# Memory results gated in the banks and summed by accumulating stores, VectorE's order written out around a chunk's sums, branch gates loaded by GpSimd

## The chip, the cores and the metric

The kernel runs on one core of one Trainium2 chip. The metric is the device time of one launch in microseconds (us). Before the change it is 2192.47 us, the median of 3 runs (2190.98 to 2194.52).

## The reference, cut to what matters

One layer for 512 positions of width 2048: a projection `h @ w_in` whose columns feed three branches, each with an output projection; the three results are weighted by sigmoid gates, added, projected once more and added to x.

```python
h = rms_norm(x, norm_g[l])
proj = h @ w_in[l]
(c_gate, b_gate, u, conv_z, c_q, c_kv, k_rope_raw, mla_z,
 mem_q, mem_z, g_conv, g_mla, g_mem) = jnp.split(proj, split_at, axis=-1)
conv_y = b_gate * causal_depthwise_conv(c_gate * u, conv_w[l])
o_conv = (conv_y * jax.nn.silu(conv_z)) @ w_conv_out[l]
mla_y = mla_attention(c_q, c_kv, k_rope_raw, cos, sin, ...)
o_mla = (mla_y * jax.nn.silu(mla_z)) @ w_mla_out[l]
mem_y = memory_attention(mem_q, mem, mem_norm_g[l], w_mem_kv[l], mem_qn_g[l], mem_kn_g[l])
o_mem = (mem_y * jax.nn.silu(mem_z)) @ w_mem_out[l]
merged = (jax.nn.sigmoid(g_conv) * o_conv + jax.nn.sigmoid(g_mla) * o_mla
          + jax.nn.sigmoid(g_mem) * o_mem)
x = x + merged @ w_o[l]
```

Everything is float32. The memory branch attends to 256 memory tokens with 4 heads; w_mem_out is 1024 x 2048, w_mla_out and w_o are 2048 x 2048.

## The kernel before

**Products.** Each float32 product is made of three matmuls (`mm3`, L158-163): weights and data are split into a high and a low part, and high x high, high x low and low x high are added up in a PSUM bank. ScalarE (ACT) writes the high part of a weight chunk, `whi`, and VectorE (DVE) the low part, `wlo = raw - whi` (L154, L155). A chunk of raw weights is a DMA of 512 KB issued by SyncE (SP). There are three `raw` buffers and two each of `whi` and `wlo`, so splits run one or two chunks ahead of the matmuls. `take()` hands out a split chunk and begins the next ones; `queue` lists all chunks of the program in order.

**Panels.** w_h, w_mla_out and w_o run as panels (`panel_steps`): 2 x 2 blocks with seven products in place of eight. VectorE first forms three sums of each raw chunk (L263-265), ACT and DVE then split seven blocks at once (`128x1792`, L268, L269). The data side needs the same: `pair_sums` (L243-246) and `pair_split` (L249 on ACT, L250 on DVE) turn a pair of 128-row blocks into a tile `xp`, `xm` or `xo`. A panel holds four banks and takes four chunks; at its end its banks are added up into a tile `e` (L304-314) and its finish function runs. w_h has 62 panels; w_mla_out and w_o have 8 each. w_mem_kv, conv_out and w_mem_out run as plain products (`dense_units`), in groups of four banks (two in w_mem_out's last two groups).

**Stages of the run**: to 106 us keys and values of the memory (w_mem_kv, with parts of x prepared beside it); to about 1343 the panels of w_h, with the rotary work at 1005 to 1025; to 1640 the latent attention; to 1700 the memory attention woven with conv_out by a table of letters (`ORDER_MEM`; `w` is a unit of conv_out); to 1735 the rest of conv_out and the splits of xm; to 1907 the panels of w_mla_out; to about 1996 w_mem_out; then w_o.

**Gates.** The sigmoid gates lie in a DRAM buffer `gdram`. conv_out's results are multiplied by their gates (`conv_result`, L1040) and stored to `mgdram` (L1041); `gate_blocks` loads the gates for it, called just before the products. w_mla_out's results are multiplied by theirs (L1217) and added to `mgdram` by an accumulating store of GpSimd (POOL), L1218; the gates `sg` for it are loaded by SP in `middle()`, which runs after `take()` of a panel's third chunk, along with the blocks `am` for w_mem_out. In w_o's panels `middle()` loads a piece of x, `xr`; at a panel's end (`finish_o`) VectorE adds to it and ACT stores it.

**Memory results** (`mem_pair`, L1231-1241): w_mem_out's five groups give eight pairs of banks. For each pair there is one tile `mg`, with a single buffer. POOL loads the gate into one half (L1233) and the merged sum of the other branches from `mgdram` into the other (L1234); VectorE multiplies the banks into the gate (L1236, two), adds (L1237), forms the pair's sums and splits (L250) into `xo`. The generator is advanced once per so many matmul units; the order on PE and SP is the order of the program text, while VectorE's, ACT's and POOL's orders are set by a scheduler, except in a region marked `manual_schedule`; before, that was VectorE in the first six chunks of w_h.

## Time and profile before

The profiled execution took 2187.3 us; its span is 2185.5 us.

| what | value |
|---|---|
| times of three runs | 2190.98, 2192.47, 2194.52 us |
| profiled execution | 2187.3 us, span 2185.5 us, mean granted clock 0.992 |
| instructions | 38852 |
| ScalarE busy | 1003.8 us |
| GpSimd busy | 123.9 us |
| DMA | 334.31 MB, mean 153 GB/s |

Spans, windows and waits are times of one profiled execution. In a window's row each engine has its busy time in that stretch, and behind it the mean TensorE clock that the throttle granted (1.00 is full) and the share of time that the 16 DMA engines were busy. A row of the waits says which engine and line waited, for what, for how long in all, how often, and the longest one. A row of a group gives its busy time and mean duration, then how long its engine sat idle before it and what ended that.

### The profile page before, as it was taken

What the parts mean: (1) busy time and instruction counts of PE and PEld (TensorE: products, weight loads), DVE (VectorE), ACT (ScalarE), POOL (GpSimd) and SP (SyncE); (2) the same over time, 40 slices, a digit from 0 to 9 for tenths busy, and PEclk for the clock granted to TensorE, in tenths of its full rate; (3) what the DMA queues carried; (4) which work ended last, traced back from release to release, by engine and by line L of the source; (5) the groups of instructions that cost most, each with busy time, mean ns of one, the idle gap of its engine ahead of it and who ended that gap; (6) DMA issues with size and microseconds to landing.
All of it is one profiled execution on the core that took longest, in us unless ns stands there. A gap on an engine that the chain in (4) does not pass through costs nothing.

```text
span 2185.5 us, 38852 instructions
## 1 busy us (share of the span) xinstructions
PE 2128.3 (97%) x16040; PEld 2038.7 (93%) x16040; DVE 1741.5 (80%) x2764; ACT 1003.8 (46%) x1219; POOL 123.9 (6%) x173
## 2 busy tenths in 40 slices
PE   9989999999999999999999999999999999998799
PEld 8789999999999999999999999888888799987799
DVE  6986888888888888888888786888877688757787
ACT  6743444344334334444444444877764433323333
POOL 0000000000000000000000001221211100000000
PEclk9999999999999999999999999999999999999899
DMA  8633433333334334343444446222266765554343
GB/s 331 231 106 136 155 136 126 126 126 129 123 126 137 115 129 137 118 141 127 136 136 139 133 136 244 74 82 108 98 231 249 306 186 173 170 204 149 126 147 136
DMA packets 92289, 334.31 MB, mean 153 GB/s; under 512 B 10768, under 2 KB 11024, under 8 KB 90064
## 3 DMA queue, kind: packets, MB, share of 16 engines
q1 hardware_dynamic: 72000, 256.77, 34.4%
q0 software_dynamic: 11616, 51.12, 6.6%
q10 hardware_dynamic: 8496, 23.94, 3.1%
q8 instruction: 125, 2.05, 0.4%
q14 instruction: 52, 0.43, 0.1%
HBM read 273.34 MB, written 58.46 MB: 152 GB/s over the span
## 4 chain that ended last, share of the span: by engine, by line
PE 81%; DVE 8%; DMA 4%; issue 4%; ACT 2%; POOL 0%; SPq 0%; DVEq 0%; POOLq 0%; ACTq 0%
PE acc L161 14%; PE acc L162 14%; PE acc L163 14%; PE aux L163 11%; PE aux L162 11%; PE aux L161 11%; DVE wlo L269 3%; DMA raw<-in_w_mla_out 1%; DMA raw<-in_w_o 1%; DVE raw L263 1%; PE aux L978 1%; DMA sb<-gdram 1%; DMA raw<-in_w_h 1%; PE aux L961 1%; DVE wlo L155 0%
## 5 line engine op out<-in xcount | busy, mean ns | idle before, releaser
L268 ACT ACTIVATE whi<-raw 128x1792 fp32r<-128x1792 f32 x304 | 517.7, 1703 | 793.0 <-PE acc L162 352.8
L269 DVE TENSOR_TENSOR wlo<-raw,whi 128x1792 fp32r<-128x1792 f32 x304 | 614.3, 2021 | 194.2 <-ACT whi L268 193.7
L163 PE MATMUL aux<-xp,wlo 128*128 128x256 f32 (+1 forms) x1712 | 479.5, 280 | 5.0 <-DVE wlo L269 5.0
L161 PE MATMUL aux<-xp,whi 128*128 128x256 f32 (+1 forms) x1712 | 479.8, 280 | 1.0 <-ACT whi L268 1.0
L162 PE MATMUL aux<-xp,whi 128*128 128x256 f32 (+1 forms) x1712 | 480.0, 280 | 0.0
L163 PE MATMUL acc<-xp,wlo 128*128 128x256 f32 x1680 | 469.4, 279 | 3.4 <-DVE wlo L269 3.4
L162 PE MATMUL acc<-xp,whi 128*128 128x256 f32 x1680 | 469.8, 280 | 0.0
L161 PE MATMUL acc<-xp,whi 128*128 128x256 f32 x1680 | 469.3, 279 | 0.0
L163 PEld LDWEIGHTS aux<-xp,wlo 128*128 128x128 f32 (+1 forms) x1712 | 320.4, 187 | 5.6 <-DVE wlo L269 5.6
L161 PEld LDWEIGHTS aux<-xp,whi 128*128 128x128 f32 (+1 forms) x1712 | 321.4, 188 | 1.4 <-ACT whi L268 1.4
L162 PEld LDWEIGHTS aux<-xp,whi 128*128 128x128 f32 (+1 forms) x1712 | 320.9, 187 | 0.0
L163 PEld LDWEIGHTS acc<-xp,wlo 128*128 128x128 f32 x1680 | 314.6, 187 | 4.3 <-DVE wlo L269 4.2
L161 PEld LDWEIGHTS acc<-xp,whi 128*128 128x128 f32 x1680 | 315.6, 188 | 0.0
L162 PEld LDWEIGHTS acc<-xp,whi 128*128 128x128 f32 x1680 | 315.1, 188 | 0.0
L263 DVE TENSOR_TENSOR raw<-raw 128x512 f32<-128x512 f32 x304 | 208.0, 684 | 57.3 <-DMA raw<-in_w_h 29.8
L155 DVE TENSOR_TENSOR wlo<-raw,whi 128x1024 fp32r<-128x1024 f32 (+2 forms) x91 | 101.5, 1119 | 47.7 <-ACT whi L154 47.7
L154 ACT ACTIVATE whi<-raw 128x1024 fp32r<-128x1024 f32 (+2 forms) x91 | 88.9, 977 | 102.6 <-PE acc L162 41.5
L265 DVE TENSOR_TENSOR raw<-raw 128x256 f32<-128x256 f32 x304 | 127.7, 421 | 6.2
L264 DVE TENSOR_TENSOR raw<-raw 128x256 f32<-128x256 f32 x304 | 127.6, 420 | 5.7
L343 POOL TENSOR_TENSOR rs_r<-rs_t,mhalf 128x2 f32<-128x2 f32 (+2 forms) x71 | 69.5, 989 | 270.0 <-DVE rs_t L342 209.6
L161 PE MATMUL acc<-whi,blk 128*128 128x384 f32 (+1 forms) x224 | 84.8, 379 | 0.0
L163 PE MATMUL acc<-whi,blk 128*128 128x384 f32 (+1 forms) x224 | 80.9, 361 | 0.0
(359 smaller groups left out, 3900.9 us busy)
## 6 DMA issues: line engine op xcount, KB each, us to landing
raw<-in_w_h SPq DMA_DIRECT2D x240, 512.0 KB, 3.5
raw<-in_w_mla_out SPq DMA_DIRECT2D x32, 512.0 KB, 3.9
raw<-in_w_o SPq DMA_DIRECT2D x32, 512.0 KB, 3.7
raw<-in_w_mem_kv SPq DMA_DIRECT2D x31, 512.0 KB, 7.2
gdram<-e ACTq DMA_DIRECT2D x22, 512.0 KB, 2.8
raw<-in_w_ukv SPq DMA_DIRECT2D x16, 512.0 KB, 5.6
raw<-in_w_conv_out SPq DMA_DIRECT2D x16, 512.0 KB, 9.0
aadram<-z POOLq DMA_DIRECT2D x8, 896.0 KB, 4.1
```

What stands on the lines that cost most here:

```text
L154: act.activation(hi[:, cols], raw[:, cols], AF.Copy)
L155: vec.tensor_tensor(out=lo[:, cols], in0=raw[:, cols], in1=r32(hi[:, cols]), op=ALU.subtract)
L161: nc.tensor.matmul(o, lhsT=s[0], rhs=m[0], start=start, stop=False, skip_group_check=shared)
L162: nc.tensor.matmul(o, lhsT=s[0], rhs=m[1], start=False, stop=False, skip_group_check=shared)
L163: nc.tensor.matmul(o, lhsT=s[1], rhs=m[0], start=False, stop=stop, skip_group_check=shared)
L263: vec.tensor_tensor(out=f[:, 4:6], in0=f[:, 1:3], in1=f[:, 0:1].to_broadcast([P, 2, 256]), op=ALU.add)
L264: vec.tensor_tensor(out=f[:, 6], in0=f[:, 5], in1=f[:, 1], op=ALU.add)
L265: vec.tensor_tensor(out=f[:, 7], in0=f[:, 6], in1=f[:, 3], op=ALU.add)
L268: act.activation(hi, f[:, 1:8], AF.Copy)
L269: vec.tensor_tensor(out=lo, in0=f[:, 1:8], in1=r32(hi), op=ALU.subtract)
L343: pool.tensor_tensor(out=r, in0=t, in1=mhalf[:, :n], op=ALU.pow)
L961: nc.tensor.matmul(sb[:, :n], lhsT=qr[:, cols], rhs=krh[:, :n], start=False, stop=False)
```

## The change

1. **Memory results.** `mem_pair` goes. `gated` multiplies two banks into a gate tile with three slots (in the place of `xo7`, which is written last); POOL then adds that to `mgdram` with an accumulating store, and `merged` loads the sum back, into places of `xo5` and `xo6` while these are not yet written. The sum on VectorE (L1237) is left out. The pair sums and the splits stand at steps of a table, `steps_out`, counted in half chunks of w_mem_out's wide groups and chunks of its narrow ones; the last two pairs are done one piece per chunk in w_o.
2. **VectorE's order** is written out from step 27 of w_mem_kv to w_h's sixth chunk, and from the beginning of w_mem_out to w_o's ninth chunk. `take()` begins the next chunk, then runs one entry of a list `fills`, where pieces of other work (x's last blocks, pair sums, results) are put.
3. **Branch gates.** The `sg` loads go from SP to POOL. `middle()` runs before `take()` of a panel's second chunk. `gate_blocks` is called ahead of the products, as soon as its pool is open.
4. **Tables.** The staging rotation of w_mem_kv, the rotary's place, `ORDER_Q1` and `ORDER_MEM` shift by a little, and `my` has four buffers in place of two.

```diff
-ORDER_MEM = "0 0 4w 1 1 4w 0 0 2 2w 1 1 3 3w 0 0 2 2 w 1 1 3 3 2w 2 2 3w 3 3 w 2 2 3 3"
+ORDER_MEM = "0 0 5w 1 1 5w 0 0 2 2w 1 1 3 2w 0 0 2 2 w 1 1 3 3 2w 2 2 2w 3 3 w 2 2 3 3"
...
     def take(ahead=1):
-        for at, entry in enumerate(queue[:2 + ahead]):
-            if entry[1] is None:
-                entry[1] = entry[0]()
-                entry.append(next(entry[1]))
-            if at <= ahead and entry[2] is None:
+        for at, entry in enumerate(queue[:1 + ahead]):
+            begin(at)
+            if entry[2] is None:
                 entry[2] = next(entry[1])
+        begin(1 + ahead)
+        if fills:
+            fills.pop(0)()
         return queue.pop(0)[2]
...
         for c in range(nch):
+            if c == 1 and middle is not None:
+                middle()
             whi, wlo = take()
             if c == 2:
                 while later:
                     later.pop(0)("aux" if tag == "acc" else "acc")
-                if middle is not None:
-                    middle()
...
+            if step == 27:
+                manual_dve.enter_context(tc.manual_schedule(engines={DVE}))
...
-    with tc.manual_schedule(engines={DVE}):
-        for step in range(6):
-            next(work)
-            if step == 0:
-                for i in (6, 7):
-                    xp.append(pair_tile(pxb, f"xp{i}"))
-                    x_load(i, etile())
-                late_parts = [x_pair(6), x_pair(7)]
-            elif step < 5:
-                for _ in range(1 + step % 2):
-                    next(late_parts[(step - 1) // 2])
+    for i in (6, 7):
+        xp.append(pair_tile(pxb, f"xp{i}"))
+        x_load(i, etile())
+        steps = x_pair(i)
+        fills += [lambda steps=steps: (next(steps), next(steps)), lambda steps=steps: next(steps)]
+    for _ in range(6):
+        next(work)
+    manual_dve.close()
...
     def conv_result(grp, banks):
-        for i, sg in enumerate(gate_blocks(grp)):
+        for i, sg in enumerate(gates_of[grp]):
...
             sgs[n] = pe.tile([P, 2, S], F32, tag="sg", name="sg", bufs=2)
-            nc.sync.dma_start(sgs[n], gdram[8 + n])
+            nc.gpsimd.dma_start(sgs[n], gdram[8 + n])
...
-    def mem_pair(n, banks):
-        t = pm.tile([P, 8, H], F32, tag="mg", name="mg", bufs=1)
-        nc.gpsimd.dma_start(two(t, 4), gdram[16 + n])
+    def gate_load(n):
+        nc.gpsimd.dma_start(gates[n % 3], gdram[16 + n])
...
+    def merged(n):
...
         nc.gpsimd.dma_start(two(t), mgdram[n])
+        mgs[n] = t
+
+    def gated(n, banks):
+        gt = gates[n % 3]
         for i in range(2):
-            vec.tensor_tensor(out=two(t, 4)[:, i], in0=banks[i], in1=two(t, 4)[:, i], op=ALU.mult)
-        vec.tensor_tensor(out=two(t), in0=two(t), in1=two(t, 4), op=ALU.add)
-        yield
-        yield from pair_parts(t, xp[n])
...
+            vec.tensor_tensor(out=gt[:, i], in0=banks[i], in1=gt[:, i], op=ALU.mult)
+        nc.gpsimd.dma_start(mgdram[n], gt, accum_op=ALU.add)
...
+    steps_out = {9: ((merged, 0), (merged, 1), (gate_load, 3), (gate_load, 4)),
+                 14: ((sums_out, 0),), 15: ((split_out, 0),), 16: ((sums_out, 1),),
+                 17: ((split_out, 1), (merged, 2), (merged, 3), (gate_load, 5), (gate_load, 6)),
+                 22: ((sums_out, 2),), 23: ((split_out, 2),), 24: ((sums_out, 3),),
+                 25: ((split_out, 3), (merged, 4), (merged, 5), (gate_load, 7)),
+                 29: ((sums_out, 4),), 30: ((split_out, 4), (merged, 6)), 31: ((sums_out, 5),),
+                 32: ((split_out, 5),)}
...
+        for i in range(width // 256):
+            gated(done + i, banks[2 * i:2 * i + 2])
...
     def finish_o(n, e):
+        fills.append(lambda: result(n, e))
+
+    def result(n, e):
...
-    for _ in work:
-        next(pairs, None)
+    merged(7)
+    fills += [lambda: None, lambda: sums_out(6), lambda: split_out(6), lambda: sums_out(7), lambda: split_out(7)]
+    for n, _ in enumerate(work):
+        if n == 8:
+            manual_dve.close()
```

How the instructions stand now: first VectorE at the beginning of w_mem_out's first narrow group, where the third wide group's banks are read. Before (the products L1236 of one pair, and its sum, pair sums and split; `raw_21825` is w_o's first chunk):

```order
L1236 TENSOR_TENSOR mg_21613<-aux_21397,mg_21613 128x512
L1236 TENSOR_TENSOR mg_21613<-aux_21398,mg_21613 128x512
L155 TENSOR_TENSOR wlo_21658<-raw_21623,whi_21657 128x512
L263 TENSOR_TENSOR raw_21825<-raw_21825 128x512
L264 TENSOR_TENSOR raw_21825<-raw_21825 128x256
L1237 TENSOR_TENSOR mg_21613<-mg_21613 128x1024
L265 TENSOR_TENSOR raw_21825<-raw_21825 128x256
L243 TENSOR_TENSOR mg_21613<-mg_21613 128x512
L244 SCALAR_TENSOR_TENSOR mg_21613<-mg_21613 128x256
L246 TENSOR_TENSOR mg_21613<-mg_21613 128x256
L155 TENSOR_TENSOR wlo_21688<-raw_21623,whi_21687 128x512
L250 TENSOR_TENSOR xo3_21258<-mg_21613,xo3_21258 128x1792
```

And of the change (L259 is the split, L252-255 are the pair sums, L1278 the products into the gate slots):

```order
L155 TENSOR_TENSOR wlo_21651<-raw_21618,whi_21650 128x512
L259 TENSOR_TENSOR xo2_21666<-mg_21568,xo2_21666 128x1792
L252 TENSOR_TENSOR mg_21570<-mg_21570 128x512
L253 SCALAR_TENSOR_TENSOR mg_21570<-mg_21570 128x256
L255 TENSOR_TENSOR mg_21570<-mg_21570 128x256
L1278 TENSOR_TENSOR gt_21263<-acc_21542,gt_21263 128x512
L1278 TENSOR_TENSOR gt_21263<-acc_21543,gt_21263 128x512
L1278 TENSOR_TENSOR gt_21263<-acc_21544,gt_21263 128x512
L1278 TENSOR_TENSOR gt_21263<-acc_21545,gt_21263 128x512
L155 TENSOR_TENSOR wlo_21693<-raw_21618,whi_21692 128x512
L259 TENSOR_TENSOR xo3_21708<-mg_21570,xo3_21708 128x1792
```

The products of all four banks now stand together right behind the group, with the sums and splits of the pairs of the group before them; the sum of mg is gone, and w_o's raw sums are later.

GpSimd's queue for the same groups, before (gate, then merged sum, for each pair), and of the change (two accumulating stores, L1279, then reload L1272 and the next gate L1259, twice):

```order
L1233 DMA mg_21703<-gdram_114 128x1024
L1234 DMA mg_21703<-mgdram_117 128x1024
L1233 DMA mg_21767<-gdram_114 128x1024
L1234 DMA mg_21767<-mgdram_117 128x1024
L1233 DMA mg_21796<-gdram_114 128x1024
L1234 DMA mg_21796<-mgdram_117 128x1024
```

```order
L1279 DMA mgdram_117<-gt_21263 128x1024 x2
L1272 DMA mg_21568<-mgdram_117 128x1024
L1259 DMA gt_21263<-gdram_114 128x1024
L1272 DMA mg_21570<-mgdram_117 128x1024
L1259 DMA gt_21263<-gdram_114 128x1024
L1279 DMA mgdram_117<-gt_21263 128x1024 x2
L1272 DMA mg_21711<-mgdram_117 128x1024
```

A store of the pair now stands between its product and its reload, and the reload of one pair stands ahead of the gate load and of the next reload.

SP's queue at w_o's third panel, before and of the change (`raw` is a chunk of w_o, `xr` the piece of x for a panel):

```order
L262 DMA raw_22266<-in_w_o 128x1024
L262 DMA raw_22332<-in_w_o 128x1024
L262 DMA raw_22383<-in_w_o 128x1024
L262 DMA raw_22434<-in_w_o 128x1024
L1277 DMA xr_22439<-in_xT 128x1024
L262 DMA raw_22487<-in_w_o 128x1024
```

```order
L271 DMA raw_22265<-in_w_o 128x1024
L271 DMA raw_22331<-in_w_o 128x1024
L1333 DMA xr_22383<-in_xT 128x1024
L271 DMA raw_22389<-in_w_o 128x1024
L271 DMA raw_22440<-in_w_o 128x1024
L271 DMA raw_22491<-in_w_o 128x1024
```

The load of xr has moved ahead of two loads of raw weights.

VectorE at the beginning of w_h, before and of the change (`wlo_980` and `wlo_968` are the first chunk's low part, `xp5` the split of x's sixth pair):

```order
L246 TENSOR_TENSOR xraw_877<-xraw_877 128x256
L265 TENSOR_TENSOR raw_945<-raw_945 128x256
L265 TENSOR_TENSOR raw_983<-raw_983 128x256
L250 TENSOR_TENSOR xp5_134<-xraw_877,xp5_134 128x1792
L269 TENSOR_TENSOR wlo_980<-raw_945,whi_979 128x1792
L269 TENSOR_TENSOR wlo_1022<-raw_983,whi_1021 128x1792
L263 TENSOR_TENSOR raw_1025<-raw_1025 128x512
```

```order
L255 TENSOR_TENSOR xraw_877<-xraw_877 128x256
L278 TENSOR_TENSOR wlo_968<-raw_947,whi_967 128x1792
L272 TENSOR_TENSOR raw_971<-raw_971 128x512
L273 TENSOR_TENSOR raw_971<-raw_971 128x256
L274 TENSOR_TENSOR raw_971<-raw_971 128x256
L259 TENSOR_TENSOR xp5_134<-xraw_877,xp5_134 128x1792
L272 TENSOR_TENSOR raw_1008<-raw_1008 128x512
L273 TENSOR_TENSOR raw_1008<-raw_1008 128x256
L274 TENSOR_TENSOR raw_1008<-raw_1008 128x256
L278 TENSOR_TENSOR wlo_1033<-raw_971,whi_1032 128x1792
```

The first chunk's low part has moved ahead of the second chunk's sums and of xp5's split; the second chunk's low part stands behind that split and behind the third chunk's sums.

More of the change, by code (lines that the diff above doesn't have):

```diff
@@ L522, in body @@
         for n in dense_units(banks, 512, mT, "T", nk=KB, before=memory_chunk if grp == 0 else None,
-                             ahead=lambda c: 2 if 0 < 8 * grp + c - 7 < 23 else 1):
+                             ahead=lambda c: 2 if 8 <= 8 * grp + c < 31 else 1):
             if n % 4 < 3:
@@ L1028, in gate_blocks @@
             out += [t[:, 0], t[:, 1]]
-        return out
+        gates_of[grp] = out
     def conv_out(grp):
@@ L1067, in conv_steps @@
                     results[grp] = r
-                    if pg is not None:
+                    if grp > 0:
                         conv_result(grp, r)
+                    if grp == 2:
+                        gate_blocks(3)
                 yield
@@ L1156, in mem_attend @@
             vec.tensor_tensor(out=z[:, f], in0=yb, in1=z[:, f], op=ALU.mult)
-            t = pq.tile([P, 2, S], F32R, tag="my", name="my", bufs=2)
+            t = pq.tile([P, 2, S], F32R, tag="my", name="my", bufs=4)
             split(z[:, f], t[:, 0], t[:, 1])
@@ L1226, in body, with place @@
     px, close_x = open_pool("xo", "right")
-    xp = [pair_tile(px, f"xo{i}") for i in range(NP)]
     pm, close_m = open_pool("merge", "right")
     pam2, close_am2 = open_pool("actm2", "left")
-    def mem_pair(n, banks):
-        t = pm.tile([P, 8, H], F32, tag="mg", name="mg", bufs=1)
-        nc.gpsimd.dma_start(two(t, 4), gdram[16 + n])
+    manual_dve.enter_context(tc.manual_schedule(engines={DVE}))
+    xp = []
+    def place(n, name):
+        return px.tile([P, 2, 7, H], F32R, tag=f"xo{n}", name=name, bufs=1)
@@ new lines, in body @@
+    gplace = r32(place(7, "gt")).rearrange("p a s n -> p (a s n)")
+    gates = [gplace[:, 1024 * i:1024 * (i + 1)].rearrange("p (f n) -> p f n", f=2) for i in range(3)]
+    mplace = {0: 6, 1: 5, 2: 6, 3: 5, 5: 6}
+    def gate_load(n):
+        nc.gpsimd.dma_start(gates[n % 3], gdram[16 + n])
+    mgs = {}
+    def merged(n):
+        if n in mplace:
+            t = r32(place(mplace[n], "mg")).rearrange("p a s n -> p (a s n)")[:, :2048]
+            t = t.rearrange("p (s n) -> p s n", s=8)
+        elif n < 7:
+            t = pm.tile([P, 8, H], F32, tag="mg", name="mg", bufs=1)
+        else:
+            t = pe.tile([P, 8, H], F32, name="mg7")
@@ L1249, in body @@
         late_blocks.append(t)
-    pairs = iter([])
-    done = 0
+    for n in range(3):
+        gate_load(n)
+    done, step = 0, 0
     for tag, width in (("acc", 512), ("aux", 512), ("acc", 512), ("aux", 256), ("aux", 256)):
@@ L1261, in body @@
             if n % 4 == 3:
-                next(pairs, None)
-        for _ in pairs:
-            pass
-        pairs = mem_pairs(done, banks)
+                step += 1
+                for do, k in steps_out.get(step, ()):
+                    do(k)
+        for i in range(width // 256):
+            gated(done + i, banks[2 * i:2 * i + 2])
         done += width // 256
@@ L1298, in tail_o @@
         nc.sync.dma_start(out[15 * P:16 * P], xr[:, 1])
-    for _ in work:
-        next(pairs, None)
+    merged(7)
[3 more added lines that the diff above has]
+            manual_dve.close()
     close_e()
```

26 lines of the change are left out of this document (20 added, 6 removed).

## The prediction

> **What bounds the kernel.** I read the page first, then the span cut into stages, then PE's waits, then the queues of the stages that lose time.
>
> ```profile
> PE 2128.3 (97%) x16040; PEld 2038.7 (93%) x16040; DVE 1741.5 (80%) x2764; ACT 1003.8 (46%) x1219; POOL 123.9 (6%) x173
> ```
>
> PE is busy for 2128.3 of 2185.5 us, and the change takes no matmul away. So all that it can win lies in PE's 57 us of idleness, and in stretches where PE ran below full clock. The table by stage (PE, PEld, DVE, ACT, POOL busy, then the granted clock, DMA share, GB/s) says where these are:
>
> ```profile
> 100.00:180.00 80.00, 71.18 (x543) 68.46 (x542) 65.42 (x90) 35.50 (x30) 1.46 (x4) 0.96 0.38 132
> 180.00:1020.00 840.00, 840.00 (x7139) 839.80 (x7139) 700.54 (x977) 351.24 (x272) 12.48 (x17) 1.00 0.39 129
> 1020.00:1045.00 25.00, 23.46 (x197) 23.06 (x197) 22.02 (x41) 12.19 (x9) 0.88 (x2) 1.00 0.43 140
> ...
> 1700.00:1760.00 60.00, 53.71 (x275) 45.77 (x274) 44.42 (x45) 26.76 (x19) 7.03 (x13) 0.94 0.77 294
> 1760.00:1900.00 140.00, 137.74 (x1161) 136.45 (x1160) 112.58 (x148) 50.28 (x35) 5.98 (x7) 1.00 0.57 174
> ...
> 1970.00:2050.00 80.00, 57.25 (x337) 50.80 (x336) 55.73 (x72) 24.50 (x19) 4.19 (x8) 0.87 0.34 123
> 2050.00:2185.00 135.00, 129.06 (x1120) 128.41 (x1119) 112.72 (x155) 45.70 (x33) 0.00 (x0) 1.00 0.44 145
> ```
>
> From 180 to 1020 us nothing can be won. The hole is 1970 to 2050, the end of w_mem_out and the beginning of w_o: 22.75 us idle. PE's waits over the whole run (total us, times, longest) name the cause:
>
> ```profile
> PE aux L161 <- DVE mg L1236: 15.0, 2, 14.4
> PE aux L163 <- DVE wlo L269: 8.3, 8, 2.2
> PE acc L163 <- DVE wlo L269: 7.2, 8, 1.6
> PE acc L161 <- DVE mg L1236: 5.7, 1, 5.7
> PE aux L163 <- DVE wlo L155: 4.7, 3, 2.8
> ```
>
> The two mg rows, 20.7 us, are w_o panels that cannot have a bank until VectorE has multiplied the gate into a memory result. GpSimd's and VectorE's rows tell why that is late:
>
> ```profile
> 1952.19 0.53 POOL L1233 DMA_DIRECT2D mg<-gdram  x1 [12.07 <-DVE xo L250]
> ...
> 1965.29 0.53 POOL L1233 DMA_DIRECT2D mg<-gdram  x1 [12.05 <-DVE xo L250]
> ```
>
> ```profile
> L1236 DVE TENSOR_TENSOR mg<-aux,mg 128x512 f32<-128x512 f32 x8 | 5.1, 685 | 9.1 <-DMA mg<-gdram 9.1
> ```
>
> The next gate is loaded only when the one mg tile has been split (xo, L250). So load, two products, sum, pair sums and split run one pair at a time, 13.1 us a pair (1965.29 - 1952.19), and the eighth pair's banks are held to the end of that queue. On top of that comes the clock:
>
> ```profile
> 2000.00:2010.00 10.00, 4.99 (x31) 4.99 (x32) 8.78 (x14) 0.00 (x0) 0.00 (x0) 0.83 0.54 200
> ...
> 2020.00:2030.00 10.00, 1.87 (x13) 1.38 (x11) 8.86 (x16) 3.40 (x2) 0.00 (x0) 0.75 0.51 188
> 2030.00:2040.00 10.00, 3.13 (x14) 3.13 (x15) 5.74 (x8) 0.00 (x0) 1.05 (x2) 0.50 0.29 105
> 2040.00:2050.00 10.00, 10.00 (x79) 10.00 (x78) 4.37 (x3) 5.10 (x3) 0.00 (x0) 0.89 0.16 54
> ```
>
> Busy time times missing clock is 0.17 x 4.99 + 0.25 x 1.87 + 0.50 x 3.13 + 0.11 x 10 = 4.0 us. So the stage loses about 27 us.
>
> **Term 1: memory results (w_mem_out and w_o).** Removed: eight sums of mg (L1237), and the hold on the banks: the gates lie loaded in three slots, and the products free the banks at once. So both mg waits go, and the 4 us of clock with them. What is late next is a longer way back: product, accumulating store, its landing, reload, pair sums, split, all in an order of VectorE that is now written by hand, so a sum that waits for its reload holds every wlo behind it, and PE waits for those. The durations:
>
> ```profile
> mgdram<-sg POOLq DMA_DIRECT2D x8, 512.0 KB, 8.5
> mg<-gdram POOLq DMA_DIRECT2D x8, 512.0 KB, 3.7
> mg<-mgdram POOLq DMA_DIRECT2D x8, 512.0 KB, 4.7
> raw<-in_w_o SPq DMA_DIRECT2D x32, 512.0 KB, 3.7
> sb<-gdram POOLq DMA_DIRECT2D x6, 512.0 KB, 7.6
> out<-xr ACTq DMA_DIRECT2D x15, 256.0 KB, 3.1
> ...
> DMA to landing us min/median/max: 2.7/7.0/9.2
> ```
>
> The first is an accumulating store of the same size to the same buffer, in the stage before; the last row is of all transfers of that buffer. From product to reloaded tile: 8.5 + 0.6 (a POOL issue) + 4.7 = 13.8 us. PE's pace is 223 matmuls in the 50 us of the first row below, 0.224 us for one of 512 columns, so 5.4 us a chunk of 24 in a wide group and 2.7 in a narrow one; a w_o chunk of 42 takes 4.8 us (42 x 40 / 355, second row):
>
> ```profile
> 1910.00:1960.00 50.00, 50.00 (x223) 41.39 (x222) 26.90 (x29) 12.85 (x11) 4.04 (x7) 1.00 0.64 221
> 2100.00:2140.00 40.00, 40.00 (x355) 40.00 (x354) 34.98 (x50) 16.13 (x11) 0.00 (x0) 1.00 0.53 171
> ```
>
> VectorE's pieces follow one another at 1.94 us for a wlo or xo of 1792 elements, 1.13 for 1024, 0.60 for 512 and 0.34 for 256, a tenth of a us less than these rows' means, since neighbours overlap:
>
> ```profile
> L269 DVE TENSOR_TENSOR wlo<-raw,whi 128x1792 fp32r<-128x1792 f32 x8 | 16.2, 2024 | 7.5 <-ACT whi L268 7.5
> ...
> L1237 DVE TENSOR_TENSOR mg<-mg 128x1024 f32<-128x1024 f32 x8 | 9.8, 1220 | 0.9 <-DMA mg<-mgdram 0.8
> ```
>
> With these I walked the new order, each row starting when its engine and its inputs are ready. As a test, the order of before, walked the same way, gives 29.8 us of waits (longest 16.0, where the trace has 14.4); with the 4.0 of clock it ends within 1 us of the trace. The new order leaves:
>
> - First narrow group: xo2 split, sums of pair 3 and four products (1.94 + 1.3 + 4 x 0.60) stand ahead of the second chunk's wlo, more than the chunk's 2.7 us; PE waits 0.9. The second narrow group: 1.2, behind xo4.
> - w_o's first three chunks: raw sums 1.3 and pair 5's sums 1.3, then xo5 and two products, lie ahead of wlo: 0.8 + 1.9 + 1.6. Then wlo, raw sums and a pair's sums or split make 1.94 + 1.3 + 1.9 = 5.1 us for a chunk of 4.8: seven times about 0.4, or 2.9.
> - Third panel: SP's load of the third xr now stands two raw loads earlier. Its buffer is free when the first panel's output is stored, which starts one chunk later than before (3.1 to land). So two raw loads are late: waits of 1.9, 2.3 and 1.7, and 2.6 later while the queue recovers.
>
> In all 18 us (0.9 + 1.2 + 4.3 + 2.9 + 5.9 + 2.6 = 17.8). None is over 2.3 us, and the waits of 95 to 185 us, at the opening of w_h, show one of 2.2 us beside a full clock:
>
> ```profile
> PE aux L163 <- DVE wlo L269: 4.1, 2, 2.2
> ...
> 140.00:150.00 10.00, 7.83 (x67) 7.63 (x66) 7.03 (x9) 3.68 (x3) 0.00 (x0) 1.00 0.28 93
> ```
>
> So term 1 is 29.8 + 4.0 - 17.8 = 16 us gained. Bounds: with an accumulate of 7 us (the median of all transfers of the buffer) the walk gives 15 us of waits, a gain of 19; with 10 (above the 9.2 seen) it gives 22.5, a gain of 11, as each further us is paid three times, at the sums of pairs 0, 2 and 4. I keep 8.5.
>
> A rule speaks against this price. The Trainium skill, "DMA: Bandwidth & Descriptors", Anatomy of one DMA, fits a GpSimd-issued transfer by 2.0 us plus its bytes over 436 GB/s: an estimate of 3.2 us for 512 KB, by which the walk would leave 15 us of waits and not 18; shorter than 7 us it buys nothing more, since the other waits do not hang on it. The trace has 8.5 for the accumulating form and 3.7 for a plain load of that size, so I go by the trace.
>
> **Term 2: opening of w_h (100 to 180).** The stage loses 8.8 us plus 0.04 x 71 = 2.8 of clock. Before, the first chunk's wlo came after both raw sums and xp5's split:
>
> ```profile
> 106.23 2.03 DVE L250 TENSOR_TENSOR xp<-xraw,xp 128x1792 fp32r<-128x1792 f32 x1 [1.16 <-ACT xp L249]
> 108.17 2.02 DVE L269 TENSOR_TENSOR wlo<-raw,whi 128x1792 fp32r<-128x1792 f32 x1
> ...
> 143.08 0.69 DVE L263 TENSOR_TENSOR raw<-raw 128x512 f32<-128x512 f32 x1 [1.30 <-DMA raw<-in_w_h]
> ```
>
> Now it precedes them: 1.94 + 1.3 us earlier, 3 us won. The third row's kind of wait, for a raw load, stays. The second chunk's wlo now stands behind xp5's split and the third chunk's raw sums, which can give the 3 back; and a clock that stays full adds up to 2. I take 3, from 0 to 5.
>
> **Term 3: conv_out's end and w_mla_out (1700 to 1900).** Lost: 6.3 us and 0.06 x 53.7 = 3.2 of clock, then 2.3. At 1714 the products (L1040) wait for a gate load and stand ahead of two wlo:
>
> ```profile
> 1714.38 1.29 DVE L1040 TENSOR_TENSOR sb<-acc,sb 128x512 f32<-128x512 f32 x2 [3.88 <-DMA sb<-gdram]
> 1715.59 2.35 DVE L155 TENSOR_TENSOR wlo<-raw,whi 128x1024 fp32r<-128x1024 f32 x2
> ```
>
> The new gate loads are issued a group earlier, and one wlo stands ahead of the products: most of the 2.8-us wait on wlo L155 and part of the clock, 3 us; at least 0, if a DMA share of 0.77 delays the earlier loads just as much, at most 4.5. The sg loads leave SP for POOL, so the raw loads of w_mla_out come earlier: 1 of the 2.3. The rotary's shift by a panel may give 0.5 of the 1.5 us idle at 1020 to 1045. Everything else that moves (staging, ORDER_Q1) lies where PE is never idle: nothing, as long as the raw loads stay ahead, and at most a wait like the 1.6 above if not.
>
> **Sum.** 16 + 3 + 3 + 1.5 = 23.5 us. The profiled execution took 2187.3; the median is 2192.5, 5.2 above it. 2187.3 - 23.5 = 2163.8; on the median's scale **2169.0**.
>
> **Rivals.**
>
> - *The way back is short.* Accumulates land in 7 us or less. For it: the DMA share is 0.34 from 1970 on, against 0.57 in the stage where the 8.5 was measured; against it: the first four fall into 1910 to 1960, where it is 0.64. Term 1 is 19 and terms 2 and 3 at their upper ends are 11: 30 us, 2162; down to 2155 if the waits at the third panel do not come either. Chance 0.22.
> - *The waits only change their name.* Accumulates go out in pairs, each a read and a write, beside the raw loads; at 10 to 11.5 us the walk leaves 22.5 to 27, a gain of 11 to 7; with terms 2 and 3 at 2 in all the time is 2179 to 2184. Against it: no transfer of the buffer took over 9.2. Chance 0.15.
> - *It does not do what it says*: w_h's and conv_out's order moves waits only, terms 2 and 3 are nothing: 2176. Chance 0.13.
> - *Slower.* VectorE's fixed order hands every us of a late reload to PE three times. The gain of 23.5 is used up at 8.5 + 23.5 / 3 = 16.3 us an accumulate. At 18 us the time is 2169 + 3 x 9.5 = 2197.5. For it: the six sb loads, as large, took 7.6 us where plain mg loads take 3.7, in a stage with twice the DMA share (0.77); twice 8.5 would do it. Against it: no stage ahead comes near that share. Chance 0.03.
>
> The Trainium skill, "DMA: Bandwidth & Descriptors", Rules for kernel authors, says that an accumulate reads its destination and writes it later, so that another access of the same bytes must wait for it. That keeps the way back serial here; GpSimd's queue of before shows one such wait, of 8.5 us, at the first mg load.
>
> **How the numbers follow.** The forecast, 2163 to 2175, has 0.47. The range takes in the first three rivals: 2155 to 2183. This kernel's measurement can tell about 0.2%, 4.4 us, from no change: faster is below 2188, 0.92; same 0.05, half of it from the second rival at its worst; slower 0.03.
>
> **What would show it.** Right: no wait of PE on gate products; clock near 1.0 from 1970 on; PE's remaining waits there all on wlo, each under 3 us, about 18 in sum; at 140 to 150 little change. Wrong: PE waiting over 3 us in a row for wlo or whi behind sums that wait for a reload (rival 2); accumulates of 5 us (rival 1); no late raw load behind the third xr (my third-panel 8 us is then too high); new waits of PE between 180 and 1640.

## The result and the profile after

The changed kernel takes 2173.19 us, the median of four runs (2168.46 to 2174.51), beside 2191.72 us for four runs of the kernel before (2186.58 to 2194.52). The ratio is 0.9914, with a 95% interval of 0.989 to 0.9939: faster by 0.6 to 1.1%. The forecast was 2169.0, its range 2155 to 2183. The profiled execution took 2174.51 us, the longest of the four, where that of before was one of the shorter ones of its kernel, so the two profiles differ by 12.8 us and the medians by 18.5. (The profiled execution of one experiment, the first below, was disturbed: of that kernel only the times are used.)

The page's first part, of the changed kernel (busy time, share of the span, instructions):

```profile
PE 2131.1 (98%) x16040; PEld 2042.4 (94%) x16040; DVE 1735.1 (80%) x2756; ACT 1003.7 (46%) x1219; POOL 135.5 (6%) x189
```

The span is 2172.7 us, so PE is idle for 41.6 us where it was 57.2. The table of stretches of the changed kernel (PE, PEld, DVE, ACT, POOL busy, granted clock, DMA share, GB/s):

```profile
100.00:180.00 80.00, 71.63 (x538) 68.67 (x537) 66.90 (x89) 35.47 (x31) 1.47 (x4) 0.96 0.39 132
...
1700.00:1760.00 60.00, 55.01 (x303) 47.66 (x302) 43.73 (x43) 27.84 (x19) 6.80 (x13) 1.00 0.82 322
1760.00:1900.00 140.00, 140.00 (x1190) 140.00 (x1190) 115.87 (x151) 49.62 (x35) 11.00 (x16) 1.00 0.64 190
1970.00:2050.00 80.00, 72.37 (x493) 65.90 (x493) 67.52 (x89) 30.09 (x24) 6.24 (x9) 0.98 0.56 161
2050.00:2172.00 122.00, 113.16 (x943) 112.35 (x941) 93.30 (x128) 38.62 (x28) 0.00 (x0) 0.99 0.41 137
```

The hole is mostly filled: from 1970 to 2050 PE issues 493 matmuls where it issued 337. The stretch behind it has become a little worse, 113.16 of 122 us busy where it was 129.06 of 135, and from 100 to 180 nothing is gained (538 matmuls; before 543). From 1760 to 1900 PE is no longer idle (137.74 of 140 us before). PE's waits, the three longest rows of the whole run (total us, times, longest; `acc` and `aux` are the two sets of PSUM banks):

```profile
PE acc L163 <- DVE wlo L278: 13.8, 13, 2.0
PE aux L163 <- DVE wlo L278: 10.4, 10, 2.2
PE aux L359 <- DVE p L1155: 2.7, 2, 2.2
```

No wait on a gate product is left. Most of what is left is waiting for low parts of weights, beside 2.7 us for a tile `p` of the memory attention, in portions of at most 2.2 us.

Since both kernels run the same matmuls, stages can be laid beside each other from the first matmul of each (us, from the traces; the memory results are w_mem_out and w_o):

| kernel | to w_h | w_h | attention, conv_out | w_mla_out | w_mem_out | w_o |
|---|---|---|---|---|---|---|
| before | 107.8 | 1227.7 | 404.4 | 167.9 | 90.3 | 182.7 |
| changed | 107.5 | 1230.1 | 401.6 | 163.9 | 89.6 | 175.3 |
| e2 scheduler's order | 108.0 | 1227.8 | 400.0 | 167.2 | 105.3 | 167.5 |
| e3 plain store | 107.4 | 1229.0 | 401.6 | 164.1 | 87.2 | 175.0 |
| e4 memory results alone | 110.4 | 1229.5 | 403.7 | 166.8 | 88.7 | 171.2 |
| e5 xr late | 106.7 | 1228.9 | 399.9 | 167.4 | 88.4 | 171.4 |
| e6 by hand to the end | 109.6 | 1228.5 | 399.9 | 164.4 | 91.5 | 181.8 |
| e7 sums first | 106.9 | 1229.5 | 399.9 | 167.9 | 88.4 | 164.6 |
| e8 all mended | 107.9 | 1221.4 | 411.8 | 165.3 | 88.0 | 163.0 |
| e9 all mended, 2 | 107.8 | 1228.8 | 399.9 | 163.2 | 89.5 | 162.6 |
| e10 w_mla_out by hand | 108.8 | 1230.2 | 409.4 | 174.4 | 89.1 | 162.6 |
| e11 gates late | 109.5 | 1229.9 | 402.1 | 165.8 | 90.4 | 174.4 |
| e12 sg on SP | 107.2 | 1229.2 | 399.9 | 166.1 | 88.2 | 170.4 |

A stage that an edit doesn't touch still moves by 2 us from trace to trace, w_mla_out by up to 4; less than that isn't read from one row. One cause is the clock, which the last section comes to. Another is visible in before's profile. The end of w_o, with PE never idle, in before (first row) and in the changed kernel (second):

```profile
2092.00:2181.00 89.00, 89.00 (x786) 88.85 (x784) 74.58 (x101) 31.04 (x23) 0.00 (x0) 1.00 0.46 151
2080.00:2168.00 88.00, 88.00 (x750) 88.00 (x748) 69.71 (x94) 30.08 (x22) 0.00 (x0) 1.00 0.39 132
```

The same matmuls at the same granted clock come every 113.2 ns (89 / 786) in the one and every 117.3 ns (88 / 750) in the other. That gave before's profile 3.2 us (786 x 4.1 ns) which the change had no part in.

### The profile page after: what moved, and what is told of

Same layout as the page of the kernel before. It is cut to its first block, busy times and chain, and to the rows that moved or that the text cites. A ratio compares the mean times of both kernels' runs of the same rounds, so it can differ in the third digit from the quotient of the medians.

```text
span 2172.7 us, 38855 instructions
## 1 busy us (share of the span) xinstructions
PE 2131.1 (98%) x16040; PEld 2042.4 (94%) x16040; DVE 1735.1 (80%) x2756; ACT 1003.7 (46%) x1219; POOL 135.5 (6%) x189
## 4 chain that ended last, share of the span: by engine, by line
PE 78%; DVE 6%; DMA 4%; ACT 3%; issue 3%; POOL 0%; SPq 0%; DVEq 0%; ACTq 0%; POOLq 0%
PE acc L161 13%; PE acc L162 13%; PE acc L163 13%; PE aux L163 12%; PE aux L162 12%; PE aux L161 11%; DVE wlo L278 3%; DMA xm<-aadram 1%; PE aux L988 1%; DMA mgdram<-gt 1%; DMA raw<-in_w_h 1%; ACT whi L277 1%; DVE raw L272 1%; DMA sb<-gdram 1%; PE aux L971 1%
## 5 line engine op out<-in xcount | busy, mean ns | idle before, releaser
L155 DVE TENSOR_TENSOR wlo<-raw,whi 128x1024 fp32r<-128x1024 f32 (+2 forms) x89 | 100.6, 1130 | 73.1 <-ACT whi L154 73.1
```

The lines of the kernel that those rows point to most:

```text
L155: vec.tensor_tensor(out=lo[:, cols], in0=raw[:, cols], in1=r32(hi[:, cols]), op=ALU.subtract)
```

## The experiments

The theory was this: the memory results' new way pays for most of the gain, it depends on VectorE's order written by hand, and what remains of waits in w_o comes from that order, not from the way back through DRAM. Rivals: the rest of the change carries as much; the way back (accumulating store, reload) sets the remaining waits. Ratios are to the kernel before in runs of the same call.

**e1, memory results undone**: the old `mem_pair`, its single `mg` and w_o's old loop come back, the rest stays, the new `take()` too.

```diff
-    def gated(n, banks):
...
+    def mem_pair(n, banks):
+        t = pm.tile([P, 8, H], F32, tag="mg", name="mg", bufs=1)
+        nc.gpsimd.dma_start(two(t, 4), gdram[16 + n])
...
```

> The changed kernel with the memory results as before (one mg tile, gate loaded after the split, VectorE ordered by the scheduler in w_mem_out and w_o); all other parts of the change stay. Theory A (the memory part carries the gain): PE's waits for gate products come back, about 20 us, and w_mem_out plus w_o take 273 to 277 us in place of 265; the whole is 8 to 12 us slower than the changed kernel, about 2183. Theory B (the gain comes from the parts ahead of it): within 4 us of the changed kernel, 2173, since what those parts won stays.

Measured: 2186.56 us, ratio 0.9963 [0.9946, 0.9981]. The rest alone brings about 8 us (4 to 12), the smaller part.

**e2, the scheduler's order**: the hand-written region from w_mem_out on is dropped; loads, stores and tables stay.

```diff
-    manual_dve.enter_context(tc.manual_schedule(engines={DVE}))
```

> The changed kernel with VectorE ordered by the scheduler in w_mem_out and w_o; gates in the banks and accumulating stores stay. Theory A (freeing the banks is not enough, the order written by hand is the gain): PE waits for wlo in w_mem_out's last groups and w_o's first chunks, about 25 us in all, and most of the gain of that stage is gone: 8 to 12 us slower than the changed kernel, w_mem_out plus w_o 273 or more. Theory B (the early release of the banks is the gain, the order adds little): within 4 us of the changed kernel.

Measured: 2183.01 us, 0.995 [0.9931, 0.9968]. PE's longest waits from 1900 to 2010 us, first of the changed kernel, then of e2:

```profile
PE acc L163 <- DVE wlo L278: 1.8, 2, 1.6
PE aux L163 <- DVE wlo L155: 0.9, 2, 0.7
```

```profile
PE aux L163 <- DVE wlo L155: 10.9, 4, 4.6
```

w_mem_out takes 105.3 us in place of 89.6: left to the scheduler, low parts that PE needs at once stand behind other work. So the gain rests on the written order: without it the two stages take 272.8 us, as before the change (273.0). In w_o alone the scheduler does better than the hand (167.5 against 175.3), which points at a fault of the written order there.

**e3, a plain store in place of the accumulating one** (the output then lacks the other two branches).

```diff
-        nc.gpsimd.dma_start(mgdram[n], gt, accum_op=ALU.add)
+        nc.gpsimd.dma_start(mgdram[n], gt)
```

> The changed kernel with a plain store in place of the accumulating one, so that the other two branches are left out of the merged sum. Theory A (the way back is not on the path at the measured landing of 6.7 us): the store lands in 4 to 5 us, and the time is within 3 us of the changed kernel. Theory B (the way back is what is late, paid three times as in the slower rival): 2 us shorter landings give 6 us or more.

Issue to landing of store and reload (queue, form, count, size, median us), the changed kernel first, then e3:

```profile
mgdram<-gt POOLq DMA_DIRECT2D x8, 512.0 KB, 6.7
mg<-mgdram POOLq DMA_DIRECT2D x8, 512.0 KB, 6.2
```

```profile
mgdram<-gt POOLq DMA_DIRECT2D x8, 512.0 KB, 3.1
mg<-mgdram POOLq DMA_DIRECT2D x8, 512.0 KB, 5.9
```

Measured: 2171.35 us, 0.9891 [0.987, 0.9912]. The store is 3.6 us shorter each time. The whole is 1.8 us shorter by the medians and 5 by the ratios, whose intervals overlap. In the stages that it touches, w_mem_out and w_o, the profile has 262.2 us in place of 264.9, where 3.6 paid three times, as the slower rival has it, would be 10.8. PE's waits on low parts of w_o stay as they were: from 1900 us on they are 7.9 + 3.1 us in the changed kernel and 8.0 + 3.2 in e3 (acc + aux). So the way back does not set these waits, and its rival falls. A gain of 2 or 3 us by a shorter store isn't excluded.

**e4, memory results alone**: every other part undone (the `sg` loads on SP, `middle()` after the third chunk's `take()`, the old opening of w_h, the old tables and gate loads). The new `take()` stays, since the results hang on its list `fills`. One of the lines, against the changed kernel:

```diff
-            nc.gpsimd.dma_start(sgs[n], gdram[8 + n])
+            nc.sync.dma_start(sgs[n], gdram[8 + n])
```

> The kernel before with the memory part alone (the openings of w_h, conv_out's gates, the sg loads, ORDER_Q1, ORDER_MEM and the rotary as before). Theory A (the parts add up): 9 to 13 us faster than before, w_mem_out plus w_o at 265 as in the changed kernel, all stages ahead as before. Theory B (the parts need each other, since the earlier sg and raw loads prepare w_mem_out): under 6 us faster.

Measured: 2173.16 us, 0.99 [0.9876, 0.9923]: as good as the whole change, which is 0.9914. The parts do not seem to add: by their ratios about 8 us for the rest (4 to 12) and 22 for this (17 to 27), against 19 for both (13 to 24). The table shows where a part of it goes: w_o takes 171.2 here and 175.3 with the rest of the change, whose `middle()` also moves the load of xr in w_o.

**e5, xr late**: `middle()` of w_o's panels alone goes back behind the third chunk's `take()`.

```diff
-            if c == 1 and middle is not None:
+            if c == 1 and middle is not None and not xr_late:
...
+                if middle is not None and xr_late:
+                    middle()
```

> The changed kernel, with w_o's xr loads back behind the third chunk (two raw loads later on SP). Theory A (as in the prediction: the third xr load waits for a store and holds two raw loads): the waits of 2.1, 1.9, 1.4 and 2.3 us after 2044 us go but for one; w_o takes about 171 us in place of 175. Theory B (they come from the scheduler's first choice after the hand-written region, two raw sums ahead of a wlo): they stay, w_o 174 to 176.

**e6, by hand to the end**: VectorE's written order runs to w_o's last chunk, not its ninth; xr as in the change.

```diff
-        if n == 8:
+        if n == 31:
```

> The changed kernel with VectorE's hand-written order kept to the end of w_o; xr stays early. Theory A (the xr load is the cause): the waits at the third panel stay, w_o 174 to 176. Theory B (the scheduler's first choice is the cause): they go but for the first (1.7 us), small waits of 0.2 to 0.5 us per chunk take their place to the end: w_o 174 to 176 as well, but with no wait over 2 us and no clock under 1.00.

At w_o's third panel the changed kernel shows the load that waits: SP's queue and ScalarE's store of the first panel (start, length, engine, line, operation), then VectorE's waits for raw loads from 2030 to 2075 us:

```profile
2042.13 0.95 ACTq L1343 DMA_DIRECT2D out<-xr  x2
```

```profile
2045.31 0.33 SPq L1333 DMA_DIRECT2D xr<-in_xT  x1
2045.75 8.74 SPq L271 DMA_DIRECT2D raw<-in_w_o  x3
```

```profile
DVE raw L272 <- DMA raw<-in_w_o: 6.1, 4, 2.9
```

SP can issue xr only when the store of 2042.13 has landed (its queue waits 10.5 us for that), and the raw loads stand behind it. PE's waits from 2062 to 2169 us, in the changed kernel, e5 and e6, in this order:

```profile
PE aux L163 <- DVE wlo L278: 2.1, 1, 2.1
```

```profile
PE aux L163 <- DVE wlo L278: 0.5, 1, 0.5
PE acc L163 <- DVE wlo L278: 0.4, 1, 0.4
```

```profile
PE aux L163 <- DVE wlo L278: 4.6, 11, 0.8
PE acc L163 <- DVE wlo L278: 3.3, 8, 0.8
```

From 2035 to 2062 us the waits on wlo add up to 5.9 us in the changed kernel, 3.6 in each of the two. Measured: e5 2170.37 us, 0.9894 [0.9878, 0.991], w_o 171.4; e6 2178.89 us, 0.9928 [0.9901, 0.9956], w_o 181.8. So two things have a part in the waits at the third panel, a late raw load and the scheduler's choices of what VectorE does first beside it: taking either away takes about half of the changed kernel's 5.9 + 2.1 = 8.0 us. But e6 carries a small wait into nearly every chunk up to the end, nineteen of them. The written order has a fault of its own, repeated in each chunk.

**e7, sums first**: in w_o `take()` begins the next chunk (raw sums, high part) before it queues the low part of the present one; by hand to the end, as e6.

```diff
     def take(ahead=1):
+        if sums_first:
+            begin(1 + ahead)
...
+            sums_first.append(1)
...
-        if n == 8:
+        if n == 31:
```

> Hand-written to the end, and in w_o a chunk's raw sums stand ahead of the wlo of the chunk before, in place of behind it. Theory A (the 0.4 us at each chunk is a ring: wlo of a chunk, raw sums of the next, its whi on ACT, its wlo, 1.9 + 1.3 + 1.7 + 0.3 = 5.2 us against PE's 4.95): the row of 0.4-us waits goes, w_o 169 to 171. Theory B (as the prediction had it: VectorE has more work per chunk than PE): the same work in another order, so they stay, w_o about 175.

Two chunks of w_o on VectorE in the changed kernel, then the ScalarE row between them:

```profile
2004.72 2.02 DVE L278 TENSOR_TENSOR wlo<-raw,whi 128x1792 fp32r<-128x1792 f32 x1 [1.91 <-ACT whi L277]
2006.66 0.68 DVE L272 TENSOR_TENSOR raw<-raw 128x512 f32<-128x512 f32 x1
...
2007.84 0.43 DVE L274 TENSOR_TENSOR raw<-raw 128x256 f32<-128x256 f32 x1
...
2010.18 2.02 DVE L278 TENSOR_TENSOR wlo<-raw,whi 128x1792 fp32r<-128x1792 f32 x1 [0.39 <-ACT whi L277]
```

```profile
2008.44 1.71 ACT L277 ACTIVATE whi<-raw 128x1792 fp32r<-128x1792 f32 x1 [3.75 <-DVE raw L274]
```

And the same place in e7:

```profile
2003.38 2.02 DVE L282 TENSOR_TENSOR wlo<-raw,whi 128x1792 fp32r<-128x1792 f32 x1 [0.16 <-ACT whi L281]
...
2006.84 0.69 DVE L276 TENSOR_TENSOR raw<-raw 128x512 f32<-128x512 f32 x1
...
2008.44 2.03 DVE L282 TENSOR_TENSOR wlo<-raw,whi 128x1792 fp32r<-128x1792 f32 x1
```

```profile
2006.70 1.70 ACT L281 ACTIVATE whi<-raw 128x1792 fp32r<-128x1792 f32 x1 [3.35 <-PE acc L162]
```

In the changed kernel the rows close a ring: low part (2004.72 to 2006.66), the next chunk's raw sums (to 2008.27), its high part on ScalarE (2008.44 to 2010.15), low part at 2010.18: 5.46 us, where PE needs 42 x 0.1173 = 4.9. The idle times say it, ScalarE waiting for the raw sums and VectorE for the high part. In e7 the sums stand a chunk further ahead: ScalarE waits only for PE to free its buffer, the low part is never late, and from 2001 to 2035 us PE has no wait on it. Measured: 2164.46 us, 0.9864 [0.9845, 0.9883], w_o 164.6.

**e8, all mended**: e7 with the late xr, each panel's result a `take()` later, pair 5's split in w_o, w_o's first raw sums begun earlier, and sums first also from w_mem_kv's step 27 to w_h's sixth chunk.

```diff
-        fills.append(lambda: result(n, e))
+        fills.extend([lambda: None, lambda: result(n, e)])
...
+                if step == 29:
+                    begin(3)
...
+                sums_first.append(1)
```

> All of it together, and the same order of raw sums at the opening of w_h: sums first, xr late, hand-written to the end, results two chunks later, pair 5's split moved behind w_o's second wlo, w_o's first raw sums two steps earlier. Theory A (waits on order alone, no engine short of time): about 2 us of waits left in w_mem_out and w_o, these 252 to 256 us in place of 265, and 2 to 4 us less in w_h's opening: 2158 to 2163. Theory B (VectorE or the raw loads are the bound there): over 2168.

Measured: 2164.2 us, 0.987 [0.9855, 0.9884], no better than e7, though w_h falls to 1221.4 and w_o to 163.0. The longest of PE's waits that take it back, and SP's row that sets it (SP had waited 19.2 us for a store `gdram<-e`):

```profile
PE aux L161 <- DMA blk<-latdram: 4.2, 1, 4.2
```

```profile
1335.31 1.75 SPq L849 DMA_DIRECT2D blk<-latdram  x4
```

The blocks for the stage behind w_h are loaded into a slot that a panel's tile `e` had; with the order of e8 it is the last panel's, whose store ends late. The attention's stage takes 411.8.

**e9, all mended, 2**: sums first ends with w_h's third chunk (n counts from 0).

```diff
+        if n == 2:
+            sums_first.clear()
```

> As the run before it, but with the sums-first order in w_h ended after its second chunk, so that the tile of the first latent block no longer takes the slot of the last panel's store. Theory A (the 8 us won in w_h and the 10 us lost at 1325 to 1350 are two separate things, the second an accident of the order in which slots rotate): w_h keeps about 1221.5 to 1222, the stage of attention and conv_out comes back to 400 to 402 with no wait of PE over 2.5 us on the latent blocks at 1325 to 1350, w_o stays at 163; the time is 2153 to 2157. Theory B (they hang together: what w_h gains only brings the panels sooner to a queue that is not ready, and the later stage pays it back): the wait at 1325 to 1350 stays in another place or w_h goes back to 1229, and the time stays at 2162 to 2166.

Measured: 2158.93 us, 0.9856 [0.9833, 0.988]: under the changed kernel by its whole interval, the fastest kernel here. Neither theory holds as written. The same loads are issued early again (e9's SP), and the attention's stage is 399.9:

```profile
1322.18 3.25 SPq L850 DMA_DIRECT2D blk<-latdram  x6
```

But w_h is back at 1228.8. A part of the reason is seen on VectorE at 139 to 145 us, in e9 and then in e8:

```profile
140.97 0.69 DVE L276 TENSOR_TENSOR raw<-raw 128x512 f32<-128x512 f32 x1 [3.15 <-DMA raw<-in_w_h]
...
142.04 2.02 DVE L282 TENSOR_TENSOR wlo<-raw,whi 128x1792 fp32r<-128x1792 f32 x1
```

```profile
139.19 2.02 DVE L282 TENSOR_TENSOR wlo<-raw,whi 128x1792 fp32r<-128x1792 f32 x1
142.25 0.69 DVE L276 TENSOR_TENSOR raw<-raw 128x512 f32<-128x512 f32 x1 [1.04 <-DMA raw<-in_w_h]
```

In e9 a low part stands behind raw sums whose load is late, and waits out the 3.15 us with them; in e8 it is done before the load is waited for. Such waits make about half of the 7.4 us: from 100 to 1330 us PE waits 8.2 us in e9 and 4.7 in e8. Most of the other half is the clock. e9 misses 0.17 x 10 us of it at 140 to 150 and (0.07 + 0.27) x 10 at 160 to 180, 5.1 in all; e8 only 0.17 x 10 at 220 to 230. An order that has e8's opening and e9's slots was not run.

**e10, w_mla_out by hand**: e9 with VectorE's order written from the end of conv_out through w_mla_out's ninth chunk.

```diff
+    manual_dve.enter_context(tc.manual_schedule(engines={DVE}))
...
+        if n == 8:
+            manual_dve.close()
```

> The kernel e9 with VectorE's order written by hand also from the end of conv_out through w_mla_out's first nine chunks, where after the change PE still waits three times 1.5 to 3.3 us behind VectorE waits of up to 5 us for a raw load that has a ready low part queued behind it. Theory A (those waits are choices of the scheduler, as in w_mem_out): the stage of w_mla_out shortens by 3 to 6 us against e9 and the waits of PE on wlo at 1740 to 1760 fall below 1 us each; the time is 3 to 6 us under e9. Theory B (the raw loads themselves are late there, the DMA share being 0.8): VectorE waits for the same loads in any order, PE's waits stay or move within a few us, and the time is within 2 us of e9.

Measured: 2178.91 us, 0.9947 [0.9928, 0.9966], 20 us behind e9, worse than either theory. PE's waits from 1700 to 1812 us and VectorE's rows before the first of them, in e10:

```profile
PE acc L163 <- DVE wlo L282: 8.9, 5, 5.6
PE acc L163 <- DVE wlo L155: 5.3, 1, 5.3
```

```profile
1710.34 2.02 DVE L263 TENSOR_TENSOR xm<-xm 128x1792 fp32r<-128x1792 f32 x1 [10.53 <-ACT xm L262]
1712.28 1.22 DVE L155 TENSOR_TENSOR wlo<-raw,whi 128x1024 fp32r<-128x1024 f32 x1
```

As written, a low part of conv_out stands behind a split of xm whose data isn't there yet, and VectorE idles 10.5 us before both. It is the mechanism of the slower rival, in another place: a fixed order hands one late transfer to all that is queued behind it.

**e11, gates late**: conv_out's gates loaded just before their products again, the old `ORDER_MEM`, two buffers of `my`.

```diff
-        for i, sg in enumerate(gates_of[grp]):
+        for i, sg in enumerate(gate_blocks(grp)):
```

> The changed kernel with conv_out's gates loaded just before their products again, the table of the memory attention as before, and two buffers of my. Theory A (term 3: the earlier gate loads are what made the end of conv_out shorter): the products at about 1710 wait 3 to 4 us for a gate load again, PE waits 2.5 to 3 us on a wlo of conv_out, and the stage from the end of w_h to w_mla_out takes 404 to 405, 3 us more than in the changed kernel. Theory B (the difference between those stages is the pace of the matmuls in one run or another): the stage stays at 400 to 402 though the products wait.

Measured: one run of 2178.78 us. From 1640 to 1760 us PE waits in e11

```profile
PE aux L163 <- DVE wlo L155: 2.7, 1, 2.7
PE aux L359 <- DVE p L1151: 1.4, 4, 0.6
```

The wait on wlo L155 is back as theory A has it, but the stage takes 402.1, 0.5 more than in the changed kernel, and not 404 to 405. For in the changed kernel PE waits 2.7 us for `p` in place of 1.4, 2.2 of them at one place, and behind that place its clock falls (the last section has the rows). The new table and gates take a wait away and give half of it back.

**e12, sg on SP**: the `sg` loads on SP and `middle()` behind the third chunk's `take()` everywhere.

```diff
-            nc.gpsimd.dma_start(sgs[n], gdram[8 + n])
+            nc.sync.dma_start(sgs[n], gdram[8 + n])
```

> The changed kernel with the gates of w_mla_out loaded by SP and the panels' middle step a chunk later, as before the change; in w_o that makes the third xr load late as well. Theory A (term 3's second part: the raw loads of w_mla_out come earlier when SP does not issue the gates): w_mla_out takes 167 to 168, 3 to 4 us more than the 163.9 of the changed kernel, with waits of VectorE for raw loads there; w_o takes about 171, as with the late xr load alone. Theory B (w_mla_out differs between runs whatever SP issues, as 164 to 168 of the runs so far suggest): it takes 164 to 165, and no wait for a raw load is longer than in the changed kernel.

Measured: one run of 2167.84 us; w_o 170.4, as with the late xr alone. w_mla_out takes 166.1, between the two theories, where kernels that load sg with GpSimd (all but before, e4 and e12) span 163.2 to 167.9, e10 left out. What SP's relief is worth stays open; it is under the spread of that stage.

## Why the prediction was right, and where it was not

**The hole**, term 1's main part: right. The waits on gate products are gone, and with them the low clock behind them; but the clock fell in two other places, as term 1's size shows.

**What is late next**: right in places, and close in sum partly by luck. In w_mem_out and w_o the changed kernel loses 17.3 us to waits, counted from start to start of its matmuls against their own pace; the walk had 17.8. The seven times 0.4 (measured: six of 0.40) and the raw loads behind the third xr are there. Of the 4.3 us at w_o's first three chunks only 0.8 and 1.6 came, by PE's wait rows.

Two reasons were off. The 0.4 was put down to VectorE's work in a chunk, 5.1 us against PE's 4.8 (42 x 40 / 355 is 4.7; at the changed kernel's pace it is 4.9). Low parts of the changed kernel, behind the one at 2010.18 that e7's rows show:

```profile
2015.63 2.02 DVE L278 TENSOR_TENSOR wlo<-raw,whi 128x1792 fp32r<-128x1792 f32 x1
...
2026.54 2.03 DVE L278 TENSOR_TENSOR wlo<-raw,whi 128x1792 fp32r<-128x1792 f32 x1
...
2031.99 2.02 DVE L278 TENSOR_TENSOR wlo<-raw,whi 128x1792 fp32r<-128x1792 f32 x1 [1.91 <-ACT whi L277]
```

Between 2010.18 and 2015.63 a split of xo stands, and VectorE is never idle: there its work does fill the 5.45 us (the raw sums took 1.5 us, not the walk's 1.3). But from 2026.54 to 2031.99 it has no such work, idles 1.91 us, and the low parts are 5.45 us apart as well. So the ring through ScalarE sets that length even without the work. e7 does the same work without the waits: its low parts are 5.06 us apart and, with a split between, 5.40 (2008.44 to 2013.84). That is still more than PE's 4.9, so e7 lives on its lead there, and more chunks of that kind would use it up. The other reason: the third panel's waits were put down to the load alone; e6 shows that the scheduler's order after the ninth chunk has a part as well.

**Term 1's size**: forecast 16, measured 8.1 (90.3 + 182.7 before, 89.6 + 175.3 after). The step of the sum that failed is the loss of before, 29.8 + 4.0. From start to start that stage lost 31.2 us, and its end ran at the faster pace, which gave back 3.2; so only 28.0 could be won. The test of the walk, "within 1 us of the trace", could not show it, since waits that were too long made up for the pace. The other step is the clock: none was to be lost, as no wait passed 2.3 us. The changed kernel, behind a wait of 1.6 us and one of 2.1 (the clock is the third number from the end):

```profile
1990.00:1995.00 5.00, 2.61 (x12) 1.74 (x11) 4.51 (x7) 3.29 (x2) 0.43 (x1) 0.98 0.83 261
1995.00:2000.00 5.00, 5.00 (x31) 5.00 (x32) 4.93 (x7) 1.70 (x1) 0.34 (x1) 0.68 0.43 158
...
2070.00:2075.00 5.00, 2.86 (x17) 2.65 (x17) 4.97 (x7) 1.70 (x1) 0.00 (x0) 0.83 0.40 112
2075.00:2080.00 5.00, 5.00 (x38) 5.00 (x37) 2.93 (x5) 0.80 (x1) 0.00 (x0) 0.83 0.62 206
```

At 0.68 and 0.83, twice, the time lost is 0.32 x 5.00 + 0.17 x (2.86 + 5.00) = 2.9 us; by the matmuls' starts it is 2.6. So 28.0 - 17.3 - 2.6 = 8.1.

**The accumulating store**: forecast 8.5 + 0.6 + 4.7 = 13.8 from product to reloaded tile, measured 6.7 + 0.6 + 6.2 = 13.5. The sum agrees by luck: two of its terms were off by 1.8 and 1.5, in opposite directions. The rival of the short way back had its condition come true (7 us or less), but not its time: e3, with 3.1 us, gains little more, as the walk said that shorter than 7 buys nothing. The fit of the Trainium skill, "DMA: Bandwidth & Descriptors", Anatomy of one DMA, gives an estimate of 3.2 us for 512 KB: the plain store of e3 agrees with 3.1, the accumulating one with its 6.7 doesn't. The wait of 8.5 us that the prediction read as the reload's stands at the gate load, L1233, which reads another buffer. The reload's own wait for the store is seen in the changed kernel, where L1272 waits three times for `mgdram<-gt`, 12.2 us in all.

**Term 2**, the opening of w_h: forecast 3, measured nothing. PE's waits from 100 to 180 us on wlo are 4.6 + 2.8 us after, 4.1 + 2.7 before. The first chunk's low part did come earlier (from 100 to 110 us PE issues 55 matmuls where it issued 32), and later chunks paid it back. The rows of e8 and e9 say why: the raw load is late, and the change left a low part queued behind its sums (VectorE waits 2.84 us there in the changed kernel, at 142). For this case the prediction had 0 as its lower bound. e8's w_h is 8.7 us under the changed kernel's, about half by shorter waits and most of the rest by the clock.

**Term 3**: forecast 4.5, measured 2.8 in the attention and conv_out, and 4.0 in w_mla_out, and that is the spread of that stage. Kernels without the early gates take 402.1 to 404.4 (before, e4, e11), those with them 399.9 to 401.6, e8 and e10 left out. A gain of 2 to 3 us is shown for the first half, none for the second.

**The sum**: 2163.8 forecast in the profile's frame, 2174.5 measured, 10.7 over: 7.9 from term 1, 5.4 from w_h (3 not won, and 2.4 lost), 2.3 back from term 3 and 0.3 ahead of w_h. Of the 2.4, 1.7 is clock: in w_h the changed kernel misses 5.1 us of it ((0.07 + 0.27) x 10 at 160 to 180, 0.34 x 5 at 230 to 235), before 3.4 (0.17 x 10 at 110 to 120 and at 170 to 180). The medians are only 4.2 us apart, since before's profile was a short run of its kernel and the profile after a long one; that the forecast comes that close is luck. Of the rivals, that of waits which only change their name holds for w_h's opening and, in half, for conv_out's end; not for the memory results.

## What to carry to other kernels

Where splits run through two engines, write out the ring (low part, next sums, high part, low part) and compare its length with the matmuls of a chunk; moving the sums one chunk ahead won 14 us (e6 to e7), a store cut to half its time 2.7 in the stages that it touches (e3). Put what is ready ahead of what waits for a load. Where the written order keeps to that, as in w_mem_out, it is worth 15.7 us (e2: 105.3 against 89.6); where it doesn't, as in e10, it costs 20. And test a walk of the schedule wait by wait and with the pace of that very run, since an end that agrees can hide two errors.
